# Pre-norm weights multiplied into the rows ahead of the transposes, with later constants and mixing weights, in a two-layer fp32 mixer kernel

## The chip, the cores and the metric

The kernel runs on one core of a Trainium2 chip. The core has five engines that work through queues of their own: TensorE (PE; PEld is its weight load), VectorE (DVE), ScalarE (ACT), GpSimd (POOL) and SyncE (SP), which here issues the DMAs. The metric is device time in microseconds (us) of one execution.

## The reference

Two layers of a model with 512 rows of 1024 numbers, in fp32. In each layer the rows are normalised and projected, three mixers work on parts of the projection, and their gated sum is projected again and added to the rows:

```
xn = rmsnorm(x, pre_g[l])            # x * rsqrt(mean(x*x) + eps) * pre_g
proj = xn @ w_in[l]                  # u, v, z, q_down, kv_down, k_rope, q, k, v, gates
y_a = sgu_mixer(u_a, v_a, ...) * silu(z_a)      # layernorm(v), lower-triangular mixing weights
y_b = mla_mixer(qd_b, kvd_b, kr_b, ...) * silu(z_b)
y_c = chunk_band_mixer(q_c, k_c, v_c, ...) * silu(z_c)
merged = sum over n of sigmoid(gates_n) * (y_n @ w_branch[l, n])
x = x + rmsnorm(merged @ w_out[l], post_g[l])
```

## The kernel before

The 512 rows are four row blocks (tb 0 to 3) of 128. Every fp32 operand of a matmul is split into a high part and a rest (hi and lo), and each product is three matmuls: hi by hi, hi by lo, lo by hi (`mm3`, L112 to L115). The normalised rows, transposed, are held as `A_h` and `A_l`, by row block; `norm_x` (L154) makes them, one row block at a call: two squares on ACT (L160), the root of the mean on DVE and POOL (L135, L136), two scalings of the rows on DVE (L164, to a tile `tmp`), eight transposes on PE (L167, to PSUM tiles `pt`), and for each of the eight transposed squares one ACT copy with the pre-norm weight as a factor (L172, `A_h`) and one DVE instruction for the rest (L173, `A_l`).

A weight piece is loaded into one of three slots `wraw` (512 KB each), cast by ACT to one of four slots `whi` (L102), and its rest is taken by DVE or POOL to one of four slots `wlo` (L107). A slot of `wraw` is free again when that rest is taken, and the next load in SP's queue waits for it.

The order of the work in a layer is: `mla_down`, four units (one for each row block) of 24 matmuls of 416 columns against the four pieces of `wqd`; the loading and masking of the mixing weights of the gated unit (`sgu_w`, L279: a load of `sgu_wt` to a `wraw` slot, a select on POOL, a cast on ACT, a rest on DVE, to `PT_h` and `PT_l`); `sgu_v`, four units of 512 columns; then one half of `z` (24 matmuls, weights `wfm`), the rope part of the mla queries and its v (weights `wrv`, results copied out of PSUM by ACT: L504 and L399), the other half of `z`, and so on. `sgu_u`, whose weights are the next four pieces `wtm`, comes behind. At the end of a layer, `W_out` has two halves (hf 0 and 1) of four units; in the second half the rows of each block are finished (L730 the square, L732 the product with the post-norm weight, L740 the addition) and layer 0 calls `norm_x` for layer 1 as soon as a block is done.

The order of the instructions in each engine's queue is set at build time by a scheduler, which keeps to the data and to the slots of each kind of tile; `after()` (L92) adds an order between two instructions. Tiles of one tag share slots: `tmp` has 3, `qk` 12, `bk` 2, the PSUM tags `pm` 3 and `pt` 2.

Of the kernel before, what the change touches and what calls it, by code (L numbers as in the profile page):

```python
# [40 lines left out]
def trunk_kernel(ctx, tc, x, wtm, wqd, wrv, wqk, wfm, wgate, wbr, wout,  # L41
# [56 lines left out]

    def split_raw(raw, cols, pool, first=None):
        hi = wp.tile([P, 1024], F32R, name="whi", tag="whi", bufs=4)  # L100
        lo = wp.tile([P, 1024], F32R, name="wlo", tag="wlo", bufs=4)
        s_.copy(out=hi[:, :cols], in_=raw[:, :cols])  # L102
        e = v_
        if pool:
            cnt[0] += 1
            e = g_ if cnt[0] % 2 == 0 else v_
        i = e.tensor_tensor(out=lo[:, :cols], in0=raw[:, :cols], in1=f32(hi[:, :cols]), op=ALU.subtract)  # L107
        if first is not None:
            after(i, first)
# [43 lines left out]

    def norm_x(tb, c):  # L154

        xr = x_rows(tb)
        ss = small("ss", 2)
        j = tmp_t()
        for hf in range(2):
            s_.activation(out=j, in_=xr[:, hf, :], func=AF.Square, scale=D ** -0.5, accum_out=ss[:, hf:hf + 1])  # L160
        r = rstd_rows(ss)
        for hf in range(2):
            xs = tmp_t()
            i = v_.tensor_scalar(out=xs, in0=xr[:, hf, :], scalar1=r[:, 0:1], scalar2=None, op0=ALU.mult)  # L164
            pt = tpsum()
            for k in range(4):
                t_.transpose(pt[:, k * P:(k + 1) * P], xs[:, k * P:(k + 1) * P], ident)  # L167
            for k in range(4):
                d = hf * 4 + k
                sl = (slice(None), d, slice(tb * P, (tb + 1) * P))  # L170
                pg = c["pre"][:, d:d + 1]
                s_.activation(out=A_h[sl], in_=pt[:, k * P:(k + 1) * P], func=AF.Copy, scale=pg)  # L172
                v_.scalar_tensor_tensor(out=A_l[sl], in0=pt[:, k * P:(k + 1) * P], scalar=pg,  # L173
                                        in1=f32(A_h[sl]), op0=ALU.mult, op1=ALU.subtract)
        return i

# [55 lines left out]
    def gate_units(l, c, i, ys, last):  # L232

        for m in range(KT):
# [20 lines left out]
            yield 2.56  # L255

    def sgu_v(l):
        lng = wk.tile([P, S], F32, name="lng", tag="zs", bufs=2)
# [4 lines left out]
        for tb in range(TB):  # L263
# [10 lines left out]
            hi, lo = x_pair(tb)  # L274
            s_.copy(out=hi, in_=vn)
            v_.tensor_tensor(out=lo, in0=vn, in1=f32(hi), op=ALU.subtract)
            yield 5.1

    def sgu_w(l):  # L279
        raw = wp.tile([P, 1024], F32, name="wraw", tag="wraw", bufs=3)  # L280
        nc.sync.dma_start(out=raw, in_=sgu_wt[l])

        g_.affine_select(out=raw.rearrange("p (g t) -> p g t", g=H), in_=raw.rearrange("p (g t) -> p g t", g=H),
                         pattern=[[0, H], [1, P]], compare_op=ALU.is_ge, fill=0.0, base=0, channel_multiplier=-1)
        wh, wl = PT_h[:, 0:1024], PT_l[:, 0:1024]
# [175 lines left out]

    def mla_down(l, st, raws, first=None):
        pc = [split_raw(raws[j], 832, False, first) if j < len(raws) else split_w(wqd[l, j], 832, False) for j in range(4)]
        for tb in range(TB):
            ps = tm_unit(pc, 416, tb)
            ss = small("ss", 2)
# [130 lines left out]
    first = norm_x(0, cl[0])
    norm_x(1, cl[0])
    dgen = None

    for l in range(L):
# [113 lines left out]
        for tb in range(TB):  # L715
            nc.sync.dma_start(out=x_rows(tb), in_=xsrc[tb * P:(tb + 1) * P, :].rearrange("p (a b) -> p a b", a=2))
        for hf in range(2):
            po = [split_w(wout[l, hf, j], 1024, False) for j in range(4)]
            for tb in range(TB):
# [19 lines left out]
                for k, src in enumerate((YT[:, tb, :], o)):  # L739
                    v_.scalar_tensor_tensor(out=xr[:, k, :], in0=src, scalar=r[:, 0:1], in1=xr[:, k, :],  # L740
                                            op0=ALU.mult, op1=ALU.add)
                    nc.sync.dma_start(out=xdst[tb * P:(tb + 1) * P, k * 512:(k + 1) * 512], in_=xr[:, k, :])
        if l < L - 1:
            st1 = {}
            dgen = mla_down(l + 1, st1, [])
            step(dgen)
            norm_x(TB - 1, cl[l + 1])

# [79 lines left out]
```

## Time and profile before

| | us |
|---|---|
| median of 3 runs | 1083.02 (1082.94 to 1084.35) |
| the profiled execution | 1083.43 |
| its span in the trace | 1081.7 |
| PE busy | 1058.4 (98%) |
| DVE busy | 651.6 (60%) |
| ACT busy | 528.7 (49%) |
| POOL busy | 235.2 (22%) |

The profiled execution has 1.7 us outside its span. PE busy counts the time in which a matmul is under way; matmuls overlap, so it says where PE stood still, and not how fast it was. The mean granted clock of TensorE is 0.998 of full speed (2.4 GHz).

### The profile page before, as it was taken

The numbers are of one execution on the slowest core, as the hardware profiler recorded it, in microseconds if no ns is written. First come the engines' busy times: TensorE is split into PE (matmuls) and PEld (weight loads), VectorE is DVE, ScalarE is ACT, GpSimd is POOL, SyncE is SP. The second block draws the span as 40 slices with busy tenths as digits, with TensorE's granted clock in tenths as the row PEclk, the third lists the DMA queues.
The fourth block names the chain that finished last, engine by engine and source line by source line (L and its number), as shares of the span: only waits on it lengthen the run. The fifth ranks groups of instructions, "written<-read, shape, count | busy, mean of one in ns | idle before, by whom it ended". The sixth has DMA issues, their size and how long they took to land.

```text
span 1081.7 us, 14177 instructions
## 1 busy us (share of the span) xinstructions
PE 1058.4 (98%) x5096; PEld 885.9 (82%) x5096; DVE 651.6 (60%) x1332; ACT 528.7 (49%) x1073; POOL 235.2 (22%) x249
## 2 busy tenths in 40 slices
PE   6999999999999999999999999999999999999997
PEld 5887878888888888888788888788888888888886
DVE  5774786666466664345577757775655666634443
ACT  6444575545454553224463645664544545432331
POOL 2311132221123232210033111331212323221000
PEclk9999999999999999999999999999999999999999
DMA  7231123223232333334342322222223322223342
GB/s 242 79 101 54 61 87 97 71 88 107 77 89 83 86 95 107 92 109 170 106 136 88 112 73 69 88 59 88 90 77 108 90 83 84 98 85 98 108 155 78
DMA packets 37703, 104.65 MB, mean 97 GB/s; under 512 B 5376, under 2 KB 6400, under 8 KB 37632
## 3 DMA queue, kind: packets, MB, share of 16 engines
q1 hardware_dynamic: 37632, 103.74, 30.9%
q8 instruction: 40, 0.66, 0.3%
q14 instruction: 31, 0.25, 0.1%
HBM read 99.53 MB, written 4.19 MB: 96 GB/s over the span
## 4 chain that ended last, share of the span: by engine, by line
PE 44%; ACT 3%; DVE 2%; issue 1%; DMA 1%; POOL 1%; POOLq 0%; DVEq 0%; ACTq 0%
PE pm L114 13%; PE pm L113 13%; PE pm L115 12%; PE pt L364 1%; PE po L382 1%; PE po L381 1%; ACT whi L102 0%; PE ps_s L422 0%; PE ps_s L421 0%; PE ps_s L441 0%; PE ps_s L440 0%; PE ps_s L439 0%; DMA wraw<-in_sgu_wt_dram 0%; ACT tmp L160 0%; DVE wlo L107 0%
## 5 line engine op out<-in xcount | busy, mean ns | idle before, releaser
L102 ACT CAST whi<-wraw 128x1024 fp32r<-128x1024 f32 (+3 forms) x194 | 177.5, 916 | 258.4 <-PE pm L114 158.2
L113 PE MATMUL pm<-A_h,whi 128*128 128x512 f32 x640 | 256.5, 401 | 1.3 <-DVE qa L215 1.3
L115 PE MATMUL pm<-A_h,wlo 128*128 128x512 f32 x640 | 249.7, 390 | 0.0
L114 PE MATMUL pm<-A_l,whi 128*128 128x512 f32 x640 | 249.4, 390 | 0.0
L107 DVE TENSOR_TENSOR wlo<-wraw,whi 128x1024 fp32r<-128x1024 f32 (+3 forms) x130 | 155.9, 1202 | 106.4 <-ACT whi L102 105.2
L107 POOL TENSOR_TENSOR wlo<-wraw,whi 128x1024 fp32r<-128x1024 f32 (+1 forms) x64 | 116.6, 1823 | 371.9 <-ACT whi L102 264.6
L113 PE MATMUL pm<-whi,A_h 128*128 128x512 f32 (+2 forms) x456 | 176.9, 388 | 3.2 <-ACT A_h L172 2.4
L114 PE MATMUL pm<-wlo,A_h 128*128 128x512 f32 (+2 forms) x456 | 175.0, 385 | 1.1 <-DVE wlo L107 1.1
L115 PE MATMUL pm<-whi,A_l 128*128 128x512 f32 (+2 forms) x456 | 174.6, 384 | 0.4
L115 PEld LDWEIGHTS pm<-A_h,wlo 128*128 128x128 f32 x640 | 120.1, 188 | 25.9
L113 PEld LDWEIGHTS pm<-A_h,whi 128*128 128x128 f32 x640 | 120.2, 188 | 24.2 <-DVE qa L215 1.8
L114 PEld LDWEIGHTS pm<-A_l,whi 128*128 128x128 f32 x640 | 120.5, 188 | 22.6
L113 PEld LDWEIGHTS pm<-whi,A_h 128*128 128x128 f32 x456 | 86.1, 189 | 20.7 <-ACT A_h L172 4.3
L114 PEld LDWEIGHTS pm<-wlo,A_h 128*128 128x128 f32 x456 | 86.3, 189 | 17.0 <-DVE wlo L107 3.3
L115 PEld LDWEIGHTS pm<-whi,A_l 128*128 128x128 f32 x456 | 86.1, 189 | 16.6 <-DVE A_l L173 1.9
L357 DVE TENSOR_SCALAR pp<-pp,st 128x128 f32<-128x128 f32 (+3 forms) x128 | 72.3, 565 | 3.5
L370 ACT CAST PT_h<-pt 128x128 fp32r<-128x128 f32 (+3 forms) x128 | 53.9, 423 | 31.8 <-PE pt L364 30.6
L426 DVE CUSTOM_DVE_ANT_0 pp<-ps_s,bk 128x128 f32<-128x128 f32 (+1 forms) x64 | 31.2, 487 | 58.2 <-PE ps_s L422 57.9
L371 DVE TENSOR_TENSOR PT_l<-pt,PT_h 128x128 fp32r<-128x128 f32 (+3 forms) x128 | 61.6, 481 | 6.5 <-ACT PT_h L370 5.6
L364 PE MATMUL pt<-ident,pp 128*128 128x128 f32 x320 | 55.7, 272 | 0.0
L429 ACT ACTIVATE pp<-pp,st 128x128 f32<-128x128 f32 (+1 forms) x64 | 36.0, 563 | 38.9 <-DVE st L428 38.4
L447 ACT ACTIVATE pp<-ps_s,st 128x128 f32<-128x128 f32 (+1 forms) x64 | 33.7, 527 | 35.8 <-DVE st L445 35.1
(180 smaller groups left out, 1580.8 us busy)
## 6 DMA issues: line engine op xcount, KB each, us to landing
wraw<-in_wgate_dram SPq DMA_DIRECT2D x48, 512.0 KB, 3.6
wraw<-in_wtm_dram SPq DMA_DIRECT2D x32, 512.0 KB, 3.5
wraw<-in_wfm_dram SPq DMA_DIRECT2D x32, 512.0 KB, 3.6
wraw<-in_wbr_dram SPq DMA_DIRECT2D x48, 256.0 KB, 2.6
wraw<-in_wout_dram SPq DMA_DIRECT2D x16, 512.0 KB, 3.7
bk<-in_rel_dram SPq DMA_DIRECT2D x16, 256.0 KB, 2.8
wraw<-in_wqd_dram SPq DMA_DIRECT2D x8, 416.0 KB, 4.6
mrg<-in_x_dram SPq DMA_DIRECT2D x8, 256.0 KB, 6.2
```

The lines of the kernel that those rows point to most:

```text
L102: s_.copy(out=hi[:, :cols], in_=raw[:, :cols])
L107: i = e.tensor_tensor(out=lo[:, :cols], in0=raw[:, :cols], in1=f32(hi[:, :cols]), op=ALU.subtract)
L113: t_.matmul(out=ps, lhsT=lh, rhs=rh, start=start, stop=False)
L114: t_.matmul(out=ps, lhsT=lh, rhs=rl, start=False, stop=False)
L115: t_.matmul(out=ps, lhsT=ll, rhs=rh, start=False, stop=stop)
L357: v_.tensor_scalar(out=pp[:, :n], in0=pp[:, :n], scalar1=rc, scalar2=None, op0=ALU.mult)
L364: t_.transpose(pt[:, kb * P:(kb + 1) * P], pp[:, kb * P:(kb + 1) * P], ident)
L370: s_.copy(out=dst(PT_h), in_=src)
L371: v_.tensor_tensor(out=dst(PT_l), in0=src, in1=f32(dst(PT_h)), op=ALU.subtract)
L426: v_.tensor_tensor_reduce(out=pp[:, :n], in0=ps[:, :n], in1=bias[:, S - n:S], scale=1.0, scalar=-3e38, op0=ALU.add, op1=ALU.max, accum_out=mx)
L429: s_.activation(out=pp[:, :n], in_=pp[:, :n], func=AF.Exp, bias=nm, accum_out=se)
L447: s_.activation(out=pp[:, :n], in_=ps[:, :n], func=AF.Exp, bias=nm, accum_out=se)
```

## The change

`norm_x` is divided in three. `pre_rows` puts the eight columns of `pre_g` by PE transposes of a column broadcast to 128 columns into two tiles `pre` of 128x512 (once a layer: 8 transposes, a DVE copy, an ACT copy). `norm_rows` makes the squares and the scaled rows, where the scaling is now row by root by `pre` in one DVE instruction. `norm_turn` makes the eight transposes, and takes four transposed squares at once: two ACT copies of 128x512 for `A_h`, two DVE subtractions for `A_l`.

```diff
-            xs = tmp_t()
-            i = v_.tensor_scalar(out=xs, in0=xr[:, hf, :], scalar1=r[:, 0:1], scalar2=None, op0=ALU.mult)
...
-                s_.activation(out=A_h[sl], in_=pt[:, k * P:(k + 1) * P], func=AF.Copy, scale=pg)
-                v_.scalar_tensor_tensor(out=A_l[sl], in0=pt[:, k * P:(k + 1) * P], scalar=pg,
-                                        in1=f32(A_h[sl]), op0=ALU.mult, op1=ALU.subtract)
+    def pre_rows(c, behind=None):
...
+                t_.transpose(pt[:, k * P:(k + 1) * P],
+                             c["pre"][:, hf * 4 + k:hf * 4 + k + 1].broadcast_to([P, P]), ident)
...
+    def norm_rows(tb, pre, behind=None):
...
+            v = v_.scalar_tensor_tensor(out=xs[hf], in0=xr[:, hf, :], scalar=r[:, 0:1], in1=pre[hf],
+                                        op0=ALU.mult, op1=ALU.mult)
...
+    def norm_turn(tb, rows, behind=None):
...
+            pv = pt.rearrange("p (k t) -> p k t", k=4)
+            sl = (slice(None), slice(hf * 4, hf * 4 + 4), slice(tb * P, (tb + 1) * P))
+            i = s_.copy(out=A_h[sl], in_=pv)
+            v_.tensor_tensor(out=A_l[sl], in0=pv, in1=f32(A_h[sl]), op=ALU.subtract)
```

The squares' outputs, the scaled rows, the `pre` tiles and the products of the last half take slots of the tag `qk` in place of `tmp`. At the start, the fourth piece of `wqd` comes in two halves to the `bk` tiles, and the order of the first casts, squares and transposes is written out with `after()`. The transposes of a block go into the middle of a unit (`mid`, called behind the second piece): at the start, blocks 2 and 3 into units 1 and 2 of `mla_down`; at the layer boundary, blocks 0 and 1 into units 2 and 3 of the last half, block 2 into unit 0 of `mla_down`, and block 3 behind its unit 1. The squares and products of a block of `W_out` are put behind the squares and scaled rows of the block before. Pieces 1 and 3 of layer 1's `wqd` have their rest taken on POOL.

```diff
         run(dgen)
-        sgu_w(l)
         vgen = sgu_v(l)
         step(vgen)
         run(mla_c(c, st))
         run(vgen)
+        w = sgu_w(l)
+        if l == 0:
+            cl.append(load_consts(1))
+            after(cl[1]["op"], w)
...
+            pc = [split_w(wqd[l, j], 832, 2 * (j % 2)) for j in range(4)]
...
+                    turn = (lambda i: norm_turn(tb - 2, rows[tb - 2], i)) if tb - 2 in rows else None
...
+                    if tb - 1 in rows:
+                        after(sq, rows[tb - 1][1])
+                        after(pm, rows[tb - 1][2])
...
+            dgen = mla_down(l + 1, st1, None, {0: lambda i: norm_turn(TB - 2, rows[TB - 2], i)})
             step(dgen)
-            norm_x(TB - 1, cl[l + 1])
+            step(dgen)
+            norm_turn(TB - 1, rows[TB - 1], last_m[0])
```

VectorE's queue in the first stage, from the rest of the fourth `wqd` piece to the evacuation of unit 0 of `mla_down` (L473, L474) and the rows of blocks 2 and 3, in the kernel before:

```order
L107 TENSOR_TENSOR wlo<-wraw,whi 128x832
L173 SCALAR_TENSOR_TENSOR A_l<-pt,col_104,A_h 128x128 x5
L287 TENSOR_TENSOR PT_l<-wraw,PT_h 128x1024
L173 SCALAR_TENSOR_TENSOR A_l<-pt,col_104,A_h 128x128 x2
L473 TENSOR_SCALAR YT<-pm,rs 128x256
L474 TENSOR_SCALAR YT<-pm,rs 128x128
L135 SCALAR_TENSOR_TENSOR rs<-ss 128x1
L173 SCALAR_TENSOR_TENSOR A_l<-pt,col_104,A_h 128x128
L164 TENSOR_SCALAR tmp<-mrg,rs 128x512 x2
L173 SCALAR_TENSOR_TENSOR A_l<-pt,col_104,A_h 128x128
L135 SCALAR_TENSOR_TENSOR rs<-ss 128x1
```

and in the changed kernel, from the scaled rows of block 1 to the first rests of `A_l` behind block 0:

```order
L190 SCALAR_TENSOR_TENSOR xs<-mrg,rs,pre 128x512 x2
L649 TENSOR_TENSOR wlo<-bk,whi 128x416 x2
L137 SCALAR_TENSOR_TENSOR rs<-ss 128x1
L190 SCALAR_TENSOR_TENSOR xs<-mrg,rs,pre 128x512 x2
L137 SCALAR_TENSOR_TENSOR rs<-ss 128x1
L190 SCALAR_TENSOR_TENSOR xs<-mrg,rs,pre 128x512 x2
L513 TENSOR_SCALAR YT<-pm,rs 128x256
L514 TENSOR_SCALAR YT<-pm,rs 128x128
L205 TENSOR_TENSOR A_l<-pt,A_h 128x4x128 x4
```

The eight rests of block 1 stood on both sides of the evacuation of unit 0 and ahead of all of block 3; now they are the first two of the four in the last row, behind the scaled rows of blocks 2 and 3 and the evacuation.

SyncE's queue in layer 0, from the constants to the pieces of `sgu_u`, in the kernel before:

```order
L614 DMA YT<-in_csnd_dram 128x4x32
L281 DMA wraw<-in_sgu_wt_dram 128x1024
L260 DMA lng<-in_ln_g_dram 128x512
L261 DMA lnb<-in_ln_b_dram 128x512
L90 DMA wraw<-in_wtm_dram 128x1024 x4
L90 DMA wraw<-in_wfm_dram 128x1024
L90 DMA wraw<-in_wrv_dram 128x1024
L90 DMA wraw<-in_wfm_dram 128x1024
L90 DMA wraw<-in_wqk_dram 128x384
L90 DMA wraw<-in_wtm_dram 128x1024 x4
```

and in the changed kernel:

```order
L681 DMA YT<-in_csnd_dram 128x4x32
L298 DMA lng<-in_ln_g_dram 128x512
L299 DMA lnb<-in_ln_b_dram 128x512
L90 DMA wraw<-in_wtm_dram 128x1024 x3
L210 DMA col_621<-in_cols_dram 128x43
L90 DMA wraw<-in_wtm_dram 128x1024
L319 DMA wraw<-in_sgu_wt_dram 128x1024
L90 DMA wraw<-in_wfm_dram 128x1024
L90 DMA wraw<-in_wrv_dram 128x1024
L90 DMA wraw<-in_wfm_dram 128x1024
L90 DMA wraw<-in_wqk_dram 128x384
L90 DMA wraw<-in_wtm_dram 128x1024 x4
```

The load of `sgu_wt` stands behind the four pieces of `sgu_v` and ahead of the first `wfm`; the order of the loads behind it is as it was.

ScalarE's queue in layer 0, from the last rows of `sgu_v` (L275, then L313) over the first half of `z` (L220, then L256) to the copies of the rope part and of v (L504 and L399, then L544 and L438), in the kernel before:

```order
L102 CAST whi<-wraw 128x1024 x2
L102 CAST whi<-wraw 128x384
L275 CAST X<-tmp 128x512
L102 CAST whi<-wraw 128x1024
L220 ACTIVATE tmp<-pm 128x512
L504 COPY mrg<-pm 128x256 x4
L399 CAST vt<-pm 128x8x64
```

and in the changed kernel:

```order
L102 CAST whi<-wraw 128x1024 x2
L102 CAST whi<-wraw 128x384
L313 CAST X<-tmp 128x512
L324 CAST PT_h<-wraw 128x1024
L256 ACTIVATE tmp<-pm 128x512
L544 COPY mrg<-pm 128x256
L102 CAST whi<-wraw 128x1024
L544 COPY mrg<-pm 128x256 x3
L438 CAST vt<-pm 128x8x64
```

The cast of `sgu_wt` (L324) has come in, and the cast of the first `sgu_u` piece stands behind the first of the four rope copies instead of ahead of `z`. In layer 1 the same rows stand in the same order.

VectorE's queue at the layer boundary, from the root of block 2 (L135, then L137) to the addition of block 3 (L740, then L816), in the kernel before:

```order
L135 SCALAR_TENSOR_TENSOR rs<-ss 128x1
L107 TENSOR_TENSOR wlo<-wraw,whi 128x832
L164 TENSOR_SCALAR tmp<-mrg,rs 128x512 x2
L107 TENSOR_TENSOR wlo<-wraw,whi 128x832
L173 SCALAR_TENSOR_TENSOR A_l<-pt,col_324,A_h 128x128
L732 TENSOR_TENSOR tmp<-pm,bk 128x512
L173 SCALAR_TENSOR_TENSOR A_l<-pt,col_324,A_h 128x128 x2
L135 SCALAR_TENSOR_TENSOR rs<-sso 128x1
L107 TENSOR_TENSOR wlo<-wraw,whi 128x832
L173 SCALAR_TENSOR_TENSOR A_l<-pt,col_324,A_h 128x128 x2
L740 SCALAR_TENSOR_TENSOR mrg<-YT,rs,mrg 128x512
L740 SCALAR_TENSOR_TENSOR mrg<-tmp,rs,mrg 128x512
```

and in the changed kernel, from the addition of block 2 on:

```order
L137 SCALAR_TENSOR_TENSOR rs<-sso 128x1
L816 SCALAR_TENSOR_TENSOR mrg<-YT,rs,mrg 128x512
L816 SCALAR_TENSOR_TENSOR mrg<-o,rs,mrg 128x512
L109 TENSOR_TENSOR wlo<-wraw,whi 128x832
L137 SCALAR_TENSOR_TENSOR rs<-ss 128x1
L190 SCALAR_TENSOR_TENSOR xs<-mrg,rs,pre 128x512 x2
L205 TENSOR_TENSOR A_l<-pt,A_h 128x4x128 x2
L805 TENSOR_TENSOR o<-pm,bk 128x512
L137 SCALAR_TENSOR_TENSOR rs<-sso 128x1
L109 TENSOR_TENSOR wlo<-wraw,whi 128x832
L816 SCALAR_TENSOR_TENSOR mrg<-YT,rs,mrg 128x512
```

There the scaled rows of block 2 (L190) stand ahead of the two rests of block 1 (L205), and these ahead of the product of block 3 and the rest of the third `wqd` piece (L109). GpSimd's queue, which gives the roots, had the six ahead of the select of `sgu_wt`:

```order
L107 TENSOR_TENSOR wlo<-wraw,whi 128x512 x6
L136 TENSOR_TENSOR rs<-rs,mhalf 128x1 x6
L283 AFFINE_SELECT wraw<-wraw 128x1024
L136 TENSOR_TENSOR rs<-rs,mhalf 128x1
L128 TENSOR_SCALAR rs<-ss 128x1
L129 TENSOR_TENSOR rs<-rs,mhalf 128x1
```

and now has rests of `wqd` between them:

```order
L109 TENSOR_TENSOR wlo<-wraw,whi 128x512 x6
L138 TENSOR_TENSOR rs<-rs,mhalf 128x1 x5
L109 TENSOR_TENSOR wlo<-wraw,whi 128x832
L138 TENSOR_TENSOR rs<-rs,mhalf 128x1
L109 TENSOR_TENSOR wlo<-wraw,whi 128x832
L138 TENSOR_TENSOR rs<-rs,mhalf 128x1 x2
```

The root for block 2's scaled rows is the first one behind a rest of 128x832.

## Rows read from the trace of the kernel before

**Rows 1.** The page, part 1: engine, busy us (share of the span), instructions.

```profile
PE 1058.4 (98%) x5096; PEld 885.9 (82%) x5096; DVE 651.6 (60%) x1332; ACT 528.7 (49%) x1073; POOL 235.2 (22%) x249
```

**Rows 2.** Waits of TensorE: us in total, times, longest.

```profile
PE pt L167 <- DVE tmp L164: 10.0, 5, 6.8
```

**Rows 3.** Stretches: from:to, length; busy time (instructions) by engine, granted clock, DMA share, GB/s.

```profile
500.00:520.00 20.00, 20.00 (x90) 16.57 (x89) 6.32 (x9) 5.23 (x11) 0.00 (x0) 1.00 0.31 116
```

**Rows 4.** Timeline of TensorE: start, us, engine, line, tiles, count, idle before.

```profile
6.84 1.97 PE L167 MATMUL pt<-ident,tmp 128*128 128x128 f32 x8 [6.84 <-DVE tmp L164]
...
11.06 0.71 PE L113 MATMUL pm<-whi,A_h 128*128 128x416 f32 x1 [2.25 <-ACT A_h L172]
...
533.14 1.07 PE L167 MATMUL pt<-ident,tmp 128*128 128x128 f32 x8 [0.60 <-DVE tmp L164]
...
539.95 1.31 PE L167 MATMUL pt<-ident,tmp 128*128 128x128 f32 x8 [0.27 <-DVE tmp L164]
...
548.67 1.09 PE L167 MATMUL pt<-ident,tmp 128*128 128x128 f32 x8 [0.45 <-DVE tmp L164]
...
560.29 1.09 PE L167 MATMUL pt<-ident,tmp 128*128 128x128 f32 x8 [1.82 <-DVE tmp L164]
```

**Rows 5.** Groups by line and shape: busy us, mean ns of one, idle before.

```profile
L107 POOL TENSOR_TENSOR wlo<-wraw,whi 128x1024 fp32r<-128x1024 f32 x30 | 72.7, 2424 | 154.8 <-ACT whi L102 103.2 <-PE pt L364 51.7
...
L172 ACT ACTIVATE A_h<-pt,col 128x128 fp32r<-128x128 f32 x64 | 21.5, 365 | 12.6 <-PE pt L167 7.6 <-DVE A_l L173 4.8
...
L173 DVE SCALAR_TENSOR_TENSOR A_l<-pt,col,A_h 128x128 fp32r<-128x128 f32 x64 | 20.5, 346 | 4.8 <-ACT A_h L172 4.3
...
L160 ACT ACTIVATE tmp<-mrg 128x512 f32<-128x512 f32 x16 | 10.2, 637 | 4.9 <-issue 2.3 <-DMA mrg<-in_x_dram 1.8 <-DVE mrg L740 0.6
...
L107 DVE TENSOR_TENSOR wlo<-wraw,whi 128x832 fp32r<-128x832 f32 x8 | 8.2, 1022 | 2.0 <-ACT whi L102 1.9
...
L740 DVE SCALAR_TENSOR_TENSOR mrg<-YT,rs,mrg 128x512 f32<-128x512 f32 x8 | 6.0, 751 | 4.9 <-POOL rs L136 4.9
...
L732 DVE TENSOR_TENSOR tmp<-pm,bk 128x512 f32<-128x512 f32 x7 | 4.8, 690 | 10.4 <-ACT tmp L730 9.8 <-PE pt L167 0.5 <-issue 0.2
```

**Rows 6.** Timeline at the layer boundary, one row block: ScalarE, then VectorE.

```profile
527.20 0.60 ACT L730 ACTIVATE tmp<-pm 128x512 f32<-128x512 f32 x1 [2.83 <-PE pm L115]
...
532.50 0.88 DVE L164 TENSOR_SCALAR tmp<-mrg,rs 128x512 f32<-128x512 f32 x2 [0.66 <-POOL rs L136]
```

**Rows 7.** Timeline of the first stage: ends of mla_down units 1 and 3 on ScalarE.

```profile
27.50 0.38 ACT L468 ACTIVATE tmp<-pm 128x256 f32<-128x256 f32 x1
...
37.35 0.39 ACT L468 ACTIVATE tmp<-pm 128x256 f32<-128x256 f32 x1
```

**Rows 8.** Timeline of layer 0 after sgu_v: VectorE, ScalarE, TensorE.

```profile
58.52 1.22 DVE L107 TENSOR_TENSOR wlo<-wraw,whi 128x1024 fp32r<-128x1024 f32 x1
...
66.64 1.06 ACT L102 CAST whi<-wraw 128x1024 fp32r<-128x1024 f32 x1 [0.31 <-PE pm L114]
...
68.08 0.64 ACT L504 COPY mrg<-pm 128x256 f32<-128x256 f32 x2
...
70.03 0.40 PE L113 MATMUL pm<-whi,ybh 128*128 128x512 f32 x1
```

**Rows 9.** Timeline of SyncE's queue: issues of weight loads.

```profile
42.52 0.33 SPq L90 DMA_DIRECT2D wraw<-in_wfm_dram  x1
...
61.51 7.80 SPq L90 DMA_DIRECT2D wraw<-in_wtm_dram  x4
```

**Rows 10.** DMA issues: count, KB each, median us from issue to landing.

```profile
wraw<-in_wtm_dram SPq DMA_DIRECT2D x32, 512.0 KB, 3.5
```

**Rows 11.** Stretches after the last matmul: columns as in group 3.

```profile
1075.00:1077.00 2.00, 0.45 (x4) 0.25 (x3) 0.65 (x3) 0.47 (x2) 0.19 (x1) 1.00 0.02 6
...
1078.00:1081.00 3.00, 0.00 (x0) 0.00 (x0) 0.81 (x2) 0.00 (x0) 0.00 (x0) 0.50 0.47 175
```

More of the change, by code (lines that the diff above doesn't have):

```diff
@@ L97, in after, with split_raw @@
                           reason="order in the queue")
-    def split_raw(raw, cols, pool, first=None):
+    def split_raw(raw, cols, pool, first=None, behind=None):
         hi = wp.tile([P, 1024], F32R, name="whi", tag="whi", bufs=4)
         lo = wp.tile([P, 1024], F32R, name="wlo", tag="wlo", bufs=4)
-        s_.copy(out=hi[:, :cols], in_=raw[:, :cols])
-        e = v_
-        if pool:
+        i = s_.copy(out=hi[:, :cols], in_=raw[:, :cols])
+        if behind is not None:
+            after(i, behind)
+        e = g_ if pool == 2 else v_
+        if pool == 1:
             cnt[0] += 1
@@ L152, in p_t, with f_tile @@
         return wk.tile([P, (qb + 1) * P], F32, name=f"pp{qb}", tag=f"pp{qb}", bufs=1)
-    def norm_x(tb, c):
+    def f_tile(nm):
+        return wk.tile([P, S], F32, name=nm, tag="qk", bufs=12)
+    def pre_rows(c, behind=None):
+        ts = []
+        for hf in range(2):
+            pt = tpsum()
+            for k in range(4):
+                t_.transpose(pt[:, k * P:(k + 1) * P],
+                             c["pre"][:, hf * 4 + k:hf * 4 + k + 1].broadcast_to([P, P]), ident)
+            ts.append(f_tile("pre"))
+            if hf == 0:
+                v_.tensor_copy(out=ts[hf], in_=pt)
+                continue
+            i = s_.copy(out=ts[hf], in_=pt)
+            if behind is not None:
+                after(i, behind)
+        return ts, i
@@ L460, in rope, with mla_down @@
         e.tensor_tensor(out=x2_, in0=tv[2], in1=tv[3], op=ALU.add)
[L462 to L463 removed]
+    def mla_down(l, st, pc, mid):
+        if pc is None:
+            pc = [split_w(wqd[l, j], 832, 2 * (j % 2)) for j in range(4)]
         for tb in range(TB):
[L465 removed]
+            ps = tm_unit(pc, 416, tb, mid=mid.get(tb))
             ss = small("ss", 2)
@@ L593, in trunk_kernel, with split_first, pre_behind @@
             cl = [load_consts(0)]
-            raws += [load_raw(wqd[0, j], 832) for j in range(2)]
+            raws += [[(load_raw(wqd[0, j], 832), 0, 832)] for j in range(2)]
         if tb == 1:
-            raws.append(load_raw(wqd[0, 2], 832))
-    first = norm_x(0, cl[0])
-    norm_x(1, cl[0])
+            raws.append([(load_raw(wqd[0, 2], 832), 0, 832)])
+            raws.append([(bk_t(S), k * 416, 416) for k in range(2)])
+            for t, c0, n in raws[3]:
+                nc.sync.dma_start(out=t[:, :n], in_=wqd[0, 3, :, c0:c0 + n])
+    def split_first(j, behind):
+        hi = wp.tile([P, 1024], F32R, name="whi", tag="whi", bufs=4)
+        lo = wp.tile([P, 1024], F32R, name="wlo", tag="wlo", bufs=4)
+        for t, c0, n in raws[j]:
+            cs = slice(c0, c0 + n)
+            i = s_.copy(out=hi[:, cs], in_=t[:, :n])
+            after(i, behind)
+            v_.tensor_tensor(out=lo[:, cs], in0=t[:, :n], in1=f32(hi[:, cs]), op=ALU.subtract)
+        return (hi, lo), i
+    def pre_behind(a):
+        pre.extend(pre_rows(cl[0], a))
+        return pre[0]
+    rows = {0: norm_rows(0, pre_behind)}
+    last_pre = pre.pop()
+    pre = pre[0]
+    pieces = [split_first(0, last_pre)[0]]
+    first = norm_turn(0, rows[0])
+    for j in (1, 2):
+        w, i = split_first(j, first)
+        pieces.append(w)
+    rows[1] = norm_rows(1, pre, i)
+    w, i = split_first(3, rows[1][1])
+    pieces.append(w)
+    for tb in (2, 3):
+        rows[tb] = norm_rows(tb, pre, i)
+    del raws
     dgen = None
```

65 lines of the change are left out of this document (38 added, 27 removed).

## The prediction

> **What bounds the kernel now.** I read the page's first part, then the waits of TensorE, then stretches, then the timeline of the places that the change touches. TensorE is under way in 98% of the span [rows 1], and in an undisturbed stretch it starts 90 matmuls of 512 columns in 20.00 us [rows 3], 0.222 us each. A change can therefore only win where TensorE stands still, and it loses whatever makes it stand still elsewhere. The waits for the old scaled rows are the largest, 10.0 us in five times [rows 2]: 6.84 us is the start of the program, and the four others lie at the layer boundary, 0.60, 0.27, 0.45 and 1.82 us, together 3.1 us [rows 4]. Besides these there is the 2.25 us wait for `A_h` at 11.06 [rows 4]. All else is small, so the most that the change can take away is some 5 us.
>
> **The small instructions.** A row block used 8 ACT copies of 0.365 us and, on DVE, 8 rests of 0.346 and two scalings, 0.88 us together [rows 5, 6]: 2.9 us of ACT, 3.6 of DVE. The new forms are not in the trace. An ACT copy of 512 columns has its nearest row in the square of that width, 0.637; the rest of 512 columns from PSUM in the product L732, 0.690; the scaling by `pre` in the addition L740, 0.751 [rows 5]. That gives 1.3 us of ACT and 2.9 of DVE a block. From above the new DVE rest is bounded by four of the old ones, 1.4 each (then nothing is won), from below by the old scaling of 512 columns, 0.44 (half of the 0.88); I take the product's 0.690, the nearest in width, source and kind. These engines have idle time, so what counts is the order in which they do it.
>
> **Start, about -0.4 (bounds -1 and +1).** The `pre` transposes run where TensorE waited, before 6.84. Block 0 needs 2 copies where it needed 8, so the first matmul comes at about 9.5 instead of 11.06 [rows 4]. But then ACT has the A_h copies (to 10.3), two casts (0.9 each, near the DVE rest of 1.02 of the same width), the squares of block 1 (0.64 and a readout of 0.2 each, to 13.7), two half casts and the squares of blocks 2 and 3 (to 17.8). DVE follows: scaled rows of block 1 by 15.8, the halves of the fourth piece by 16.8, and unit 0 ends at about 17.4. Now comes what the order shows: DVE does the scaled rows of blocks 2 and 3, each behind a root on POOL (0.66 of wait, two times 0.75), so until about 21, then the evacuation of unit 0, and only then the rest for block 1, at about 22.3. TensorE has done the transposes of block 1 by 18.4 and can do two matmuls of unit 1; then it waits some 4 us. With 22 matmuls of 416/512 of 0.222 us (0.18, an estimate) and one block of transposes (1.07 [rows 4]) unit 1 ends at 27.4, where ACT takes it at 27.50 today, and unit 3 at about 37, today 37.35 [rows 7]. The early gain is given back in one long gap.
>
> **Middle of each layer, +1.7 twice.** `sgu_wt` used to take a raw slot early and give it back before `sgu_v`. Now it takes one of three behind the `wtm` pieces and keeps it until its rest is taken, behind the cast that I see placed after the last X cast, near 67. The second `wfm` load, issued at 42.52 today [rows 9], must then wait for the rest of the first `wfm`, 58.52 + 1.22 = 59.74 [rows 8]. From there the chain is serial: load 3.5 (the median of the equal `wtm` loads [rows 10]), cast 1.06 (the row of 66.64 [rows 8]), rest on POOL 2.42 [rows 5]: 66.7. The first `sgu_u` load, which goes out at 61.51 today [rows 9], waits for that slot: issued 66.7, landed 70.2, cast until 71.3. By the order this cast stands on ACT ahead of the last three rope copies, which today begin at 68.08 [rows 8]; the copy of the second rope unit ends 0.3 later, and v's first matmul, at 70.03 today [rows 8], needs that PSUM slot: 71.7. So 1.7 us of standing TensorE, with nothing behind that has slack. Layer 1 has the same rows in the same order. Bounds: zero if the load comes ahead of its chain; 3.5 each if both loads take a quarter longer than the median (0.9 each). POOL's select and the casts of `sgu_wt` themselves hide under `sgu_v`, in which ACT and DVE have time; if that cover went, 1.05 us more.
>
> **Boundary, +0.7 (bounds -3 and +2).** The turned blocks come one unit later, which by itself would take away the 3.1 us. I follow the DVE queue instead. From the end of a unit of W_out to its scaled rows is 527.20 to 532.50, 5.3 us [rows 6]; the two new scalings add 1.5, and the rests of the block before, now behind them, 1.4: 8.2. As the product (ready after 0.8) begins this, DVE needs 7.4 us for a block, against TensorE's 24 times 0.222 and 1.07 for a turn, 6.4. It falls behind by one us a block, and block 2 starts its product 2.1 after its unit. Then come the rest of the first `wqd` piece (1.02 [rows 5]), and on POOL a rest of 832 columns, 2.42 times 832/1024 = 2.0, ahead of the root of block 2. Its scaled rows are done 9.8 after the unit, the rests of block 1 at 11.1. TensorE wants to turn block 2 at 6.4 + 12 times 0.18 = 8.6; its PSUM tiles come free with these rests, at 10.4 and 11.1. I count 0.4 for the POOL rest that unit 0 needs, 1.4 and 0.3 for the two tiles, and 1.0 for the rest of the third piece, which stands behind the next product: 3.1 us again. Block 3 is ready before its turn. Gain and loss cancel, and there are eight `pre` transposes more, 1.07 us by the equal row, of which I take 0.7, since some fall into the wait for the first W_out pieces.
>
> **Sum.** 1083.43 + 3.4 + 0.7 - 0.4 = 1087.1 for an execution like the profiled one, span and 1.7 us around it included. That one is 0.4 above the median of the runs, so 1086.7.
>
> **Rivals.**
> The clock falls in the first stage. After its last matmul TensorE is at 1.00 in 1075 to 1077 and at 0.50 in 1078 to 1081 [rows 11]: half speed, 1.2 GHz, after a short rest. The gap that I expect at 18.4 to 22.3, with two matmuls in it, is of that kind. At half speed the next 4 us of work would take 8 or, if only part of it is hit, 6: about +2, 1088.7. The Trainium skill's page "TensorE: Matmul & The Clock Gate", section "What's actually happening", says that the throttled state is the default and that activity releases it; by that rule a gap is paid once more after its end, as the last rows suggest. No row of this trace shows a fall between two matmuls.
> The boundary pays in full. If DVE keeps up (the new forms at their lower bounds, or POOL's rest earlier), the 3.1 us go and the sum is 1083.6: no change.
> Faster. The load chain has more room than I see: the second `wfm` lands early, or the scheduler's copies do not hold v, and the boundary pays as well. Then -0.4 at the start, -2.4 at the boundary and nothing in the middle: 1080.2. It decides at whether the first `sgu_u` cast begins before 68. Against it: each step is a slot that a row shows busy.
> The change does not do what it says: the transposed rows might still wait for the old roots; that is contained in the boundary's bounds.
>
> **How the numbers follow.** My forecast 0.42, the clock 0.20, the boundary alone 0.22, faster 0.16. A difference under 0.2% (2.2 us) is no change for this measurement: 1080.9 to 1085.2. The faster case gives 0.15 below that, the boundary case and the low end of the forecast 0.25 inside, the rest 0.60 above. The range 1081.5 to 1089.5 leaves out most of the faster case and the sum of all bad ends. The forecast alone would be 1085 to 1088.5.
>
> **What would show it.** A wait of TensorE of 1.5 to 2 us just ahead of v in both layers, behind the rope copies and a cast that waited for a DMA of `wtm`: without it, the middle term is wrong. A gap near 18 to 22 us that ends with `A_l`, and a clock below 1.00 behind it or not. At the boundary, waits of the transposes of block 2 for `A_l` and of `mla_down` for `wlo`; if TensorE runs through there, the boundary's sum is wrong. A gap at the old places would mean that nothing moved.

## The result, and the profile after

The changed kernel takes 1093.13 us (median of 5 runs, 1092.53 to 1095.08), the kernel before 1083.79 beside it: a ratio of 1.0093 with a 95% interval from 1.0078 to 1.0107. That is 9.3 us slower. The direction was forecast, the size was not: 1086.7 was the forecast, and 1089.5 the end of the range. The profiled execution took 1092.99 us, with a span of 1091.2 and a mean granted clock of 0.995.

TensorE's waits in the changed kernel (engine, line, waited for: us in total, times, longest):

```profile
PE pt L165 <- DMA col<-in_cols_dram: 4.6, 1, 4.6
PE pm L117 <- DVE A_l L205: 3.8, 1, 3.8
PE pm L115 <- ACT mrg L544: 2.5, 2, 1.3
PE pm L116 <- DVE wlo L109: 1.9, 3, 0.9
PE pm L115 <- DVE zs L258: 1.6, 2, 0.9
...
```

The 10.0 us of waits for scaled rows [rows 2] have become 0.9 (a row not shown here). The first row is the program's start. The others are new: one wait for the rests of block 1, two in each layer ahead of the fourth rope unit (for `zs`) and of v, and the waits for `wlo`, the longest of which is the second of two at the layer boundary (shown below).

To see where the time went, I take the same piece of work in both timelines. Unit 3, the last one of `mla_down`, ends in layer 0, as ScalarE takes it, in the changed kernel at

```profile
40.77 0.38 ACT L508 ACTIVATE tmp<-pm 128x256 f32<-128x256 f32 x1
```

against 37.35 [rows 7]: 3.4 us are lost in the first stage. The next three rows are TensorE's of the changed kernel: the first v matmul of layer 0, the last matmul of layer 1's `mla_down`, and the first v matmul of layer 1.

```profile
75.29 0.51 PE L115 MATMUL pm<-whi,ybh 128*128 128x512 f32 x1 [1.31 <-ACT mrg L544]
...
575.85 0.35 PE L117 MATMUL pm<-whi,A_l 128*128 128x416 f32 x1
...
611.17 0.50 PE L115 MATMUL pm<-whi,ybh 128*128 128x512 f32 x1 [1.22 <-ACT mrg L544]
```

The last two of these in the kernel before:

```profile
568.98 0.35 PE L115 MATMUL pm<-whi,A_l 128*128 128x416 f32 x1
...
602.03 0.40 PE L113 MATMUL pm<-whi,ybh 128*128 128x512 f32 x1
```

Against 70.03 [rows 8], 568.98 and 602.03 the changed kernel is 5.3, 6.9 and 9.1 us late, and its span is 9.5 us longer. By difference: first stage 3.4, middle of layer 0 1.9, from there to the end of layer 1's `mla_down` 1.6, middle of layer 1 2.3, and 0.4 behind.

The first stage by stretches (from:to, length; busy time and count of PE, PEld, DVE, ACT, POOL; granted clock; DMA share; GB/s):

```profile
18.00:20.00 2.00, 0.65 (x2) 0.30 (x2) 1.34 (x4) 0.80 (x2) 1.39 (x3) 1.00 0.88 341
20.00:22.00 2.00, 0.00 (x0) 0.00 (x0) 1.14 (x3) 0.00 (x0) 1.59 (x3) 0.92 0.27 110
22.00:24.00 2.00, 1.21 (x4) 1.16 (x4) 1.33 (x3) 0.00 (x0) 0.00 (x0) 0.50 0.04 13
24.00:28.00 4.00, 4.00 (x17) 3.78 (x15) 0.00 (x0) 0.48 (x1) 0.00 (x0) 0.50 0.00 0
28.00:30.00 2.00, 2.00 (x11) 1.97 (x10) 1.38 (x2) 0.69 (x2) 0.00 (x0) 0.88 0.03 8
```

TensorE does two matmuls in four us, and the granted clock falls to 0.50, that is 1.2 GHz, within the gap. Then PE is fully busy from 24 to 28, but at half speed. The gap's end and its cause, on TensorE and VectorE of the same kernel:

```profile
18.66 0.35 PE L116 MATMUL pm<-wlo,A_h 128*128 128x416 f32 x1
22.79 0.71 PE L117 MATMUL pm<-whi,A_l 128*128 128x416 f32 x1 [3.78 <-DVE A_l L205]
```

```profile
16.88 1.41 DVE L190 SCALAR_TENSOR_TENSOR xs<-mrg,rs,pre 128x512 f32<-128x512 f32 x2 [0.66 <-POOL rs L138]
...
19.03 1.41 DVE L190 SCALAR_TENSOR_TENSOR xs<-mrg,rs,pre 128x512 f32<-128x512 f32 x2 [0.66 <-POOL rs L138]
20.88 0.48 DVE L513 TENSOR_SCALAR YT<-pm,rs 128x256 f32<-128x256 f32 x1 [0.44 <-POOL rs L131]
...
22.05 1.28 DVE L205 TENSOR_TENSOR A_l<-pt,A_h 128x512 fp32r<-128x512 f32 x2
```

The rests of block 1 (L205) start only when the scaled rows of blocks 2 and 3 and the evacuation of unit 0 are done, as their order says.

The clock falls a second time, at the layer boundary, behind two waits with 1.4 us of work between them:

```profile
555.66 1.26 PE L199 MATMUL pt<-ident,xs 128*128 128x128 f32 x8 [1.55 <-DVE A_l L205]
...
558.02 0.71 PE L116 MATMUL pm<-wlo,A_h 128*128 128x416 f32 x1 [0.92 <-DVE wlo L109]
```

```profile
558.00:560.00 2.00, 1.98 (x6) 1.90 (x7) 1.59 (x3) 0.75 (x3) 0.38 (x1) 0.50 0.77 254
```

ScalarE in the middle of layer 0, changed kernel:

```profile
66.66 1.66 ACT L102 CAST whi<-wraw 128x1024 fp32r<-128x1024 f32 x2 [3.14 <-DMA wraw<-in_wfm_dram]
...
68.75 1.05 ACT L324 CAST PT_h<-wraw 128x1024 fp32r<-128x1024 f32 x1
70.20 0.60 ACT L256 ACTIVATE tmp<-pm 128x512 f32<-128x512 f32 x1 [0.40 <-PE pm L117]
70.85 0.37 ACT L544 COPY mrg<-pm 128x256 f32<-128x256 f32 x1
73.92 1.04 ACT L102 CAST whi<-wraw 128x1024 fp32r<-128x1024 f32 x1 [2.70 <-DMA wraw<-in_wtm_dram]
74.88 0.91 ACT L544 COPY mrg<-pm 128x256 f32<-128x256 f32 x3
```

ScalarE waits 3.14 us for the second `wfm` load and then 2.70 us for the first `sgu_u` load, with three rope copies behind the cast of that piece; v starts when the first of the three is done.

### The profile page after: what moved, and what is told of

The parts are those of the page before. It is cut to its first block, busy times and chain, and to the rows that moved or that the text cites. A ratio compares the mean times of both kernels' runs of the same rounds, so it can differ in the third digit from the quotient of the medians.

```text
span 1091.2 us, 14115 instructions
## 1 busy us (share of the span) xinstructions
PE 1063.0 (97%) x5112; PEld 892.5 (82%) x5112; DVE 649.5 (60%) x1285; ACT 518.7 (48%) x1028; POOL 239.2 (22%) x251
## 4 chain that ended last, share of the span: by engine, by line
PE 83%; ACT 4%; DVE 3%; issue 1%; DMA 1%; POOL 1%; DVEq 0%; POOLq 0%; ACTq 0%
PE pm L115 24%; PE pm L116 24%; PE pm L117 24%; PE pt L403 3%; PE po L421 2%; PE po L420 2%; ACT whi L102 1%; PE ps_s L461 1%; PE ps_s L460 1%; PE ps_s L480 1%; PE ps_s L479 1%; PE ps_s L478 1%; DMA wraw<-in_wtm_dram 1%; ACT mrg L336 1%; ACT qa L250 0%
## 5 line engine op out<-in xcount | busy, mean ns | idle before, releaser
L102 ACT CAST whi<-wraw 128x1024 fp32r<-128x1024 f32 (+3 forms) x190 | 174.1, 917 | 266.3 <-PE pm L116 158.1
L109 DVE TENSOR_TENSOR wlo<-wraw,whi 128x1024 fp32r<-128x1024 f32 (+3 forms) x124 | 152.1, 1230 | 109.6 <-ACT whi L102 108.5
L109 POOL TENSOR_TENSOR wlo<-wraw,whi 128x1024 fp32r<-128x1024 f32 (+2 forms) x66 | 120.5, 1826 | 371.3 <-ACT whi L102 264.1
L115 PE MATMUL pm<-X,whi 128*128 128x512 f32 x128 | 51.0, 399 | 0.0
```

Of the source, the lines that this page charges most:

```text
L102: i = s_.copy(out=hi[:, :cols], in_=raw[:, :cols])
```

## The experiments

Each was run beside the kernel before; the changed kernel stands at 1.0093 on this scale. Every ratio has an interval of about 0.0013 to both sides, which is given where it decides.

**Late rows.** The rows of blocks 2 and 3 are built behind the transposes of block 1.

```diff
-    for tb in (2, 3):
-        rows[tb] = norm_rows(tb, pre, i)
...
-            norm_turn(1, rows[1], last_m[0])
+            last = norm_turn(1, rows[1], last_m[0])
+            for tb in (2, 3):
+                rows[tb] = norm_rows(tb, pre, last)
```

> The squares and scaled rows of blocks 2 and 3 are built behind the transposes of block 1, so that on VectorE the rests of block 1 come first. Theory A (the first stage is lost by the clock, which falls in the wait for these rests): the wait of 3.78 us at 22.79 shrinks below 1.5, the granted clock stays at 1.00 up to 30 us, the last matmul of mla_down of layer 0 starts at about 35 instead of 40.3, and the time is 4.5 to 6 us under the changed kernel, about 1088. Rival B (VectorE's amount of work sets the first stage, not its order): the wait only moves to the transposes of blocks 2 and 3, and the time falls by less than 2 us, above 1091.

Measured: 1089.75 us, ratio 1.0061 (1.0049 to 1.0074), 3.4 us better than the changed kernel. The wait and the clock, with the end of unit 3:

```profile
20.88 0.46 PE L117 MATMUL pm<-whi,A_l 128*128 128x416 f32 x1 [1.34 <-DVE A_l L205]
```

```profile
20.00:24.00 4.00, 3.09 (x17) 2.54 (x18) 2.97 (x7) 2.06 (x7) 0.84 (x2) 1.00 0.17 63
24.00:28.00 4.00, 4.00 (x25) 3.96 (x23) 2.61 (x4) 1.70 (x7) 0.96 (x3) 1.00 0.01 4
```

```profile
36.60 0.39 ACT L508 ACTIVATE tmp<-pm 128x256 f32<-128x256 f32 x1
```

The wait is 1.34 instead of 3.78, the clock stays at 1.00, and unit 3 ends at 36.60 instead of 40.77: 4.2 us in the stage where A wanted 5.3, and 0.75 before the old 37.35 [rows 7]. The whole run wins less than the 4.5 us of A; in its trace the clock falls behind the wait for v in layer 1 (606 to 610 us), where the changed kernel's stays at 1.00, and from there to the end it is 1.9 us slower. In the first stage the order of VectorE's queue, and not its work, made the loss. Whether the wait or the clock costs it, this run can't tell, since both went.

**Fill the gap.** Sixteen matmuls into a `pm` tile that nobody reads, in the place where TensorE waits.

```diff
         i = t_.matmul(out=ps, lhsT=lh, rhs=rl, start=False, stop=False)
+        if fill:
+            junk = main()
+            for k in range(fill):
+                j = t_.matmul(out=junk, lhsT=lh, rhs=rl_fill[0], start=k == 0, stop=k == fill - 1)
+                after(j, i)
...
```

> Sixteen matmuls of 512 columns whose result nobody reads stand in TensorE's queue behind the second matmul of unit 1 of mla_down in layer 0, where TensorE waits 3.8 us; nothing else is changed. They take about 3.6 us. Theory A (the clock): the clock stays at 1.00 in 20 to 28 us, the wait for the rests is unchanged, but the matmuls behind it run at full speed, and the time falls by about 3 us to 1090. Rival B (the wait alone costs it): the time stays at 1093 or rises.

Measured: 1091.66 us, ratio 1.0076 (1.0063 to 1.0088). By the ratios that is 1.8 us better with more work, but the interval overlaps that of the changed kernel, so it is the trace that decides. The end of the gap and the clock behind it:

```profile
23.56 0.46 PE L123 MATMUL pm<-whi,A_l 128*128 128x416 f32 x1 [0.16 <-DVE A_l L216]
```

```profile
24.00:28.00 4.00, 4.00 (x27) 3.92 (x26) 1.28 (x3) 1.08 (x2) 0.00 (x0) 1.00 0.01 4
```

The matmul that waits for the rests comes no earlier (23.56 here, 22.79 there, in an execution whose first matmul came 0.4 later), yet 27 matmuls are under way at some time in 24 to 28 us instead of 17, at a clock of 1.00 instead of 0.50, and unit 3 ends at

```profile
38.91 0.39 ACT L521 ACTIVATE tmp<-pm 128x256 f32<-128x256 f32 x1
```

From the end of the gap to there it is 15.35 us; in the changed kernel 17.98. So the fallen clock costs 2.6 us by itself, and theory A holds for that much. The whole run won less than the 3 us expected: the gap ended 0.8 later, and here too the clock falls behind the wait for v in layer 1 (608 to 612 us), which makes the rest of the run 1.7 us slower than in the changed kernel.

**A place of its own for the mixing weights.** They stay late, in two tiles of the tag `qk` with a select, cast and rest each.

```diff
-        raw = wp.tile([P, 1024], F32, name="wraw", tag="wraw", bufs=3)
-        nc.sync.dma_start(out=raw, in_=sgu_wt[l])
+        for k in range(2):
+            raw = f_tile("wsg")
+            nc.sync.dma_start(out=raw, in_=sgu_wt[l, :, k * 512:(k + 1) * 512])
...
```

> The mixing weights are loaded in two halves to two tiles of the tag qk instead of a slot of wraw; they stay late. Theory A (the slot that sgu_wt keeps makes the second wfm load and the first sgu_u load late, and the cast of that piece holds the rope copies): the waits ahead of the third rope unit and of v, 2.4 us in each layer, go, and the time falls by about 4.8 us, to 1088.3. Rival B (the late cast and rest of the mixing weights hold ScalarE): these waits stay at over 1 us a layer and the time falls by less than 2.5 us.

Measured: 1088.92 us, ratio 1.0055 (1.0042 to 1.0067), 4.1 us better. ScalarE and TensorE in the middle of layer 0:

```profile
70.02 1.14 ACT L326 CAST PT_h<-wsg 128x512 fp32r<-128x512 f32 x2
71.06 1.05 ACT L102 CAST whi<-wraw 128x1024 fp32r<-128x1024 f32 x1
...
72.50 0.63 ACT L546 COPY mrg<-pm 128x256 f32<-128x256 f32 x2
```

```profile
72.91 0.38 PE L115 MATMUL pm<-whi,ybh 128*128 128x256 f32 x1 [0.69 <-ACT mrg L546]
74.44 0.40 PE L115 MATMUL pm<-whi,ybh 128*128 128x512 f32 x1
```

The cast of the `sgu_u` piece no longer waits for a DMA, it stands ahead of the copies again, and v runs without a wait. What is left, 0.69 us ahead of the third rope unit, comes from the late cast (L326), which A had not counted. From the end of `mla_down` to v this run takes 1.3 us less than the changed kernel in layer 0 and 1.4 less in layer 1, so the slot is the cause of most of what the middle loses. That is 2.7 of the 4.1 us; the first stage of this execution is 0.5 slower. Another 1.8 lie between v of layer 0 and the end of layer 1's `mla_down`, where nothing was edited: the two waits at the boundary are the same as in the changed kernel, but the clock does not fall behind them.

```profile
554.36 1.25 PE L199 MATMUL pt<-ident,xs 128*128 128x128 f32 x8 [1.55 <-DVE A_l L205]
...
556.68 0.45 PE L116 MATMUL pm<-wlo,A_h 128*128 128x416 f32 x1 [0.88 <-DVE wlo L109]
```

```profile
558.00:560.00 2.00, 2.00 (x12) 1.97 (x11) 1.74 (x4) 1.93 (x9) 0.11 (x1) 1.00 0.78 287
```

From the end of the second wait to the last matmul of `mla_down` it is 16.48 us here (556.68 to 573.16) and 17.83 in the changed kernel (558.02 to 575.85). So that theory A's 1088.3 was nearly met is in part luck, and the fallen clock at the boundary costs the changed kernel 1.35 us.

**The rests of `wqd` on VectorE.** `2 * (j % 2)` becomes `False` in layer 1's `mla_down`.

> The rests of pieces 1 and 3 of layer 1's wqd are taken on VectorE instead of GpSimd. Theory A (VectorE is the queue that is behind at the layer boundary; GpSimd's rest ahead of the root of block 2 only adds to it): the root comes 1.5 to 2 us earlier, VectorE has one us more to do ahead of it and one behind, the waits of 1.55 and 0.92 us at 555.7 and 558.0 change by less than 1 us together, time 1092 to 1093.5. Rival B (GpSimd's rest is the cause of the wait): the wait of 1.55 us goes, time about 1091.3.

Measured: 1092.12 us, ratio 1.0085 (1.0071 to 1.0099), which can't be told from the changed kernel. In the trace the waits of 1.55 and 0.92 us are now three, of

```profile
555.30 0.66 PE L199 MATMUL pt<-ident,xs 128*128 128x128 f32 x4 [0.47 <-DVE A_l L205]
556.90 0.46 PE L116 MATMUL pm<-wlo,A_h 128*128 128x416 f32 x1 [0.75 <-DVE wlo L109]
559.69 0.46 PE L116 MATMUL pm<-wlo,A_h 128*128 128x416 f32 x1 [0.44 <-DVE wlo L109]
```

1.66 in place of 2.47 us: a change of 0.8, as A had it. GpSimd's rest is a part of the wait for block 2, and what is saved there goes partly into later rests on VectorE.

**Defer.** At the boundary the squares and scaled rows of a block are written behind the next unit and its turned block.

```diff
+                    if hf == 1 and l < L - 1 and tb > 0:
+                        rows[tb - 1] = norm_rows(tb - 1, pre)
                     sq = s_.activation(out=f_tile("sq")[:, :c1 - c0], in_=ps, func=AF.Square, scale=D ** -0.5,
...
-                if l < L - 1:
-                    rows[tb] = norm_rows(tb, pre)
...
```

> Of the changed kernel only the layer boundary is altered: the squares and scaled rows of a block are written behind the unit of the next block and its turned block, so that the rests of block 1 stand on VectorE ahead of the root and scaled rows of block 2. Theory A (the wait of 1.55 us for A_l ahead of the transposes of block 2 comes from VectorE's order): that wait goes, the transposes of block 2 wait for their scaled rows at most 0.5 us, and the time falls by 1 to 2 us, to about 1091.5. Rival B (VectorE and GpSimd have too much to do there in any order): a wait as long for xs, and a time within 0.5 us of 1093.1.

Measured: 1093.47 us (4 runs), ratio 1.0087 (1.0074 to 1.0101). At the boundary the trace shows what A said:

```profile
557.38 1.29 PE L199 MATMUL pt<-ident,xs 128*128 128x128 f32 x8 [0.37 <-DVE xs L190]
560.71 0.46 PE L116 MATMUL pm<-wlo,A_h 128*128 128x416 f32 x1 [0.42 <-POOL wlo L109]
```

The waits are 0.79 together instead of 2.47, and the clock stays at 1.00 there. The time does not show it: by itself the run is within noise of 1.0093. In its traced execution the clock falls in the middle of layer 0, behind the wait for v, where the changed kernel's does not:

```profile
76.00:78.00 2.00, 2.00 (x6) 1.56 (x5) 2.00 (x7) 0.59 (x1) 0.00 (x0) 0.50 0.36 80
```

From the first v matmul at 75.31 fourteen starts take 6.09 us here and 3.35 in the changed kernel, 2.7 more, which is more than the shorter waits give. Whether the other executions of this run lost it in the same place is not on record. The mechanism is shown, its worth in time by itself is not.

**Two fixes**: the late rows, and the mixing weights in `qk` tiles and worked on during `sgu_v`.

> The rows of blocks 2 and 3 behind the transposes of block 1, and the mixing weights in two qk tiles, loaded, masked and cast during sgu_v and not behind it. Theory A (both losses are separate and add): the 3.4 us of the late rows and the 4.1 us of the slot go, and the last wait of 0.9 us a layer ahead of the rope units too, since the cast no longer stands there: 1093.1 - 3.4 - 4.1 - 1.8 = 1083.8, within 0.2% of the kernel before. Rival B (the early cast takes ScalarE from the turned blocks in the first stage): the first stage loses a us, 1085 to 1086.

Measured: 1085.1 us, ratio 1.0013 (1.0004 to 1.0023). Within the intervals the losses add: 8.0 thousandths less than the changed kernel, where the two single runs, with the last wait of each layer still in, gave 3.2 and 3.8. The time itself is the one that B named, and 1.3 us above that of A. B's cause is not shown: the trace of this run is not read here. In that of the next run, which has the same first stage, the clock falls there (0.65 at 22 to 24 us, 0.50 at 24 to 26).

**All fixes**: the two and the deferred rows.

> The two fixes and the boundary order of the run before together. Theory A (the three losses add): 1.5 us under the run with two fixes, about 1082.3, at or just under the kernel before. Rival B: the boundary's gain does not show, 1083.8.

Measured: 1082.47 us, ratio 0.9992 (0.9983 to 1.0001). Here the boundary shows: 2.1 thousandths under the two fixes, and the two intervals just do not meet. The time is the one that A named, and it can't be told from that of the kernel before.

**All fixes, and the rests of `wqd` on VectorE.**

> As the run before, with all rests of layer 1's wqd on VectorE. Theory A (GpSimd's rest ahead of the root of block 2 is the last to hold its rows): another 0.5 to 1 us less, about 1081.5. Rival B (VectorE is the queue that is behind, and two more rests there cost more than the root gains): 0.5 to 1 us more than the run before, about 1083.

Measured: 1082.48 us, ratio 0.9988 (0.9979 to 0.9997): faster than the kernel before by a little, and not to be told from the run above. At the boundary GpSimd is free, but the scaled rows come later, behind the rests on VectorE:

```profile
550.42 1.29 PE L199 MATMUL pt<-ident,xs 128*128 128x128 f32 x8 [1.74 <-DVE xs L190]
```

Neither theory's number is met; in time the two places for that work cost the same.

**The form alone.** The kernel before with only the new form of the norm: `pre` tiles, scaled rows with the weights, copies and rests of 512 columns; every load, the mixing weights and the places of the transposes as before.

> The kernel before with the new form of the norm alone: pre tiles once a layer, scaled rows with the weights, two ScalarE copies and two VectorE rests of 512 columns for a block; loads, mixing weights, constants and the places of the transposes as before. Theory A (the loss of the changed kernel is in the orders and the slot, not in the new form; the form takes about 0.7 us of VectorE and 1.6 us of ScalarE from each block): no wait of over 2.5 us behind the first matmuls of the first stage, the granted clock stays at 1.00 from 17 to 30 us, no waits ahead of v, and a time of 1081 to 1083.5, not above the kernel before. Rival B (the new form costs by itself, by longer scaled rows and 16 transposes more): 1084.5 to 1086.

Measured: 1090.55 us, ratio 1.0069 (1.0055 to 1.0082): both theories are off. TensorE in the first stage:

```profile
12.82 1.12 PE L168 MATMUL pt<-ident,tmp 128*128 128x128 f32 x4 [3.69 <-DVE tmp L164]
...
28.38 1.75 PE L168 MATMUL pt<-ident,tmp 128*128 128x128 f32 x8 [2.21 <-DVE tmp L164]
```

The scheduler puts the copy of the second `pre` tile behind three weight casts on ScalarE, the last of which waits for its DMA, so the second half of the first block is turned after a wait of 3.69 us; the squares of block 2 stand behind the cast of `sgu_wt`. Unit 3 of `mla_down` ends 3.8 us later than in the kernel before. At the boundary another 3.4 us go: four waits for scaled rows, 4.4 us together where the kernel before has 3.1, and the clock falls (0.63 and 0.52 in 564 to 568 us). The middle of both layers loses nothing. So the form costs if its order is left to the scheduler as it stands here; that it need not cost is shown by the run with all fixes.

## Why the prediction was right and wrong

**The first stage is the step that failed.** The prediction had "about -0.4" there; it was +3.4. Its sequence was right to within some 0.3 us where it counts: the first matmul at 9.17 (9.5 in the prediction), the rests at 22.05 (22.3), the wait of 3.78 ("some 4 us"). But the term took 0.18 us for each matmul behind the gap, full speed, and put the fall of the clock aside as a rival of 0.20 worth 2 us. The clock fell within the gap to 0.50, and 24 to 28 us hold 17 matmuls where the run with the filled gap has 27. Filling the gap gives 2.6 us back without any earlier rest. Of the 3.8 us between -0.4 and +3.4 that is the greater part; 0.5 is the later end of the gap (22.79 for 22.3). Of the 0.7 that are left, 0.6 is a reading: 90 is the number of matmuls that touch the 20 us of [rows 3], of which 88 start in them, so those of 512 columns start 0.228 us apart and not 0.222; those of 416 columns start 0.19 apart (28.68 to 32.65 us in 21 steps in the changed kernel) and not 0.18, and 70 of them lie behind the gap. Smaller terms, some of them of the other sign, were not told apart. The rule that the prediction cites from the Trainium skill, page "TensorE: Matmul & The Clock Gate", section "What's actually happening", that the throttled state is the default and activity releases it, agrees with these stretches: 0.50 at 22 to 28 us, and 1.00 again after TensorE had been busy since 22.79.

**The middle of each layer: mechanism right, size a little short.** 1.7 twice was forecast; 1.9 and 2.3 were measured by the landmarks. The chain is as written: load, cast, GpSimd's rest, load, cast, copy, v. From the end of the rest of the first `wfm` to v it takes 12.2 us in layer 0 (63.06 to 75.29) and 12.3 in layer 1, where the prediction's steps add to 12.0; in layer 1 that rest also ends 0.3 later behind `mla_down` than it did in the kernel before. The second wait, 0.75 and 0.90 us ahead of the fourth rope unit for `zs`, was not foreseen. On VectorE the rest of the mixing weights (1.21 us) stands ahead of `zs`. By the order of the queues this wait costs nothing more, since v is held by the copy of the second rope unit, which does not need it; no run tests that alone. The prediction let "the casts of `sgu_wt` themselves hide"; the run with a slot of their own shows what they cost when the loads no longer hide them, the 0.69 us.

**The boundary: waits right, the clock left out.** +0.7 was forecast, with 3.1 us of waits; the trace has 1.55 and 0.92 us where it counted 1.7 and 1.0, and from v of layer 0 to the end of layer 1's `mla_down` the kernel loses 1.6. The sum has no term for the clock there, and the rival of the clock speaks of the first stage alone. The clock fell to 0.50 behind the second of these waits, which costs 1.35 us against the run in which the same waits passed at 1.00. That VectorE is the engine that is behind there is borne out by the deferred rows, whose waits fall to 0.79 without less work.

**The sum.** With 3.4, 1.9, 1.6, 2.3 and 0.4 in place of -0.4, 1.7, 0.7, 1.7 and 0 the sum is 9.6 instead of 3.7; 3.8 of the 5.9 between them lie in the first stage. The fallen clock, 2.6 there and 1.35 at the boundary, is 4.0 of the 5.9. The prediction priced it as a rival of its forecast, at 2 us and for one place; it is a term, it can come at each gap, and it comes together with the middle's loss. The range left that sum out.

## What to carry to other kernels

A piece of work that is made early can stand in the way: read, for each instruction that a late engine needs next, what its queue puts ahead of it. A gap of TensorE behind which its clock may fall belongs in the sum, with the price of the matmuls behind it, and is no side case. Compare two kernels stage by stage, at the same piece of work in both: where the clock falls moves a whole run by one to three us, which is as much as one of these fixes is worth. When a transfer gets a place in a shared ring of slots, follow every later load of that ring to the first instruction that waits for it in order, and give it a place of its own if it sits for long.

## What was not expected of the hardware

The granted clock fell to 0.50 within a wait of 3.78 us with two matmuls ahead of it, and came back to 1.00 only between 28 and 30 us, after some six us of work (0.88 in that stretch). Much shorter waits did it too, and not every time. These are the stretches, counted in steps of 2 us from 16 us to the last matmul, in which the mean granted clock of the traced execution was below 0.70:

| | first stage | middle of layer 0 | boundary | middle of layer 1 |
|---|---|---|---|---|
| before | | | | |
| changed | 22 to 28 | | 558 to 560 | |
| late rows | | | 552 to 554 | 606 to 610 |
| filled gap | | | 554 to 556 | 608 to 612 |
| own place | 22 to 28 | | | |
| rests of `wqd` on VectorE | 24 to 26 | 74 to 78 | | |
| deferred rows | 24 to 26 | 74 to 82 | | |
| all fixes | 22 to 26 | | | |
| all fixes, rests on VectorE | 22 to 24 | | | |
| form alone | 28 to 32 | | 564 to 568 | |

Each lies behind a wait that the kernel before does not have there or has shorter. The wait need not be long: with all fixes the clock falls behind one of 1.34 us, as long as the one of the late rows, behind which it stays at 1.00:

```profile
21.72 0.45 PE L117 MATMUL pm<-whi,A_l 128*128 128x416 f32 x1 [1.34 <-DVE A_l L205]
```

```profile
22.00:24.00 2.00, 2.00 (x9) 1.93 (x9) 1.34 (x4) 0.62 (x3) 0.55 (x1) 0.65 0.12 44
24.00:26.00 2.00, 2.00 (x10) 1.86 (x9) 1.34 (x4) 0.28 (x1) 0.55 (x1) 0.50 0.00 0
```

What decides between the two is not shown here.

Two small instructions of VectorE lasted until GpSimd's rest beside them ended. The root of block 2 in the changed kernel took 1.43 us, where the next one took 0.32 and most take 0.15, with GpSimd's rest beside it:

```profile
551.43 1.43 DVE L137 SCALAR_TENSOR_TENSOR rs<-ss 128x1 f32<-128x1 f32 x1 [0.64 <-ACT sq L181]
```

```profile
550.86 1.99 POOL L109 TENSOR_TENSOR wlo<-wraw,whi 128x832 fp32r<-128x832 f32 x1 [2.45 <-ACT whi L102]
```

It ends with GpSimd's rest, and so does the next one (557.04 us, against 557.02 for the rest beside it). Moving work to GpSimd was then not free for VectorE here, even for an instruction of one column. In the same stretch the rests and the product that VectorE reads from PSUM kept their usual length (1.28 us for two, 0.68).
